# Hybrid encoder layer on one core: the first 256 tokens of each projection in three 256-column matmuls into half a bank

## The chip, the core and the metric

The kernel runs on one core of a Trainium2 chip as one program. The metric is device time in microseconds (us), as the median of several executions. Five engines work side by side and wait for each other through semaphores: PE (TensorE, the matrix multiplier; the trace shows its weight loads apart, as PEld), DVE (VectorE), ACT (ScalarE), POOL (GpSimd) and SP, which issues most of the transfers. PE writes its sums into PSUM, which is cut into banks of 512 fp32 columns on 128 partitions; here eight banks are dealt out by name.

## The reference

One layer of a hybrid encoder is computed for 512 prompt tokens and 64 sample tokens, 576 in all, with a model width of 1024:

```
n = rmsnorm(x);  proj = n @ w_in            (3592 columns: conv input, z, a, b, q, k, v)
oa = gated delta rule over silu(conv(...)), 4 heads;  ob = differential attention, 4 heads
h = x + [oa ; ob] @ w_out
h = h + memory attention(rmsnorm(h) @ w_mem_q, memory K/V) @ w_mem_o
h = h + (relu(rmsnorm(h) @ w_ff1) ** 2) @ w_ff2      (4096 hidden columns)
y = rmsnorm(h)
```

All of it is fp32, and K, V, states and convolution tails are returned too. Every product with a large weight matrix is a *projection* below.

## The kernel before, in words

**Split operands.** A projection does not multiply fp32 by fp32. Weights and activations are each split into a high part, rounded to the format fp32r, and a low part, the rounded remainder: `wh`, `wl` for weights, and the high and low halves of an operand tile `x`. A product is then three fp32r matmuls: wh·x_high, wh·x_low and wl·x_high. ACT makes a high part by a copy, DVE a low part by a subtraction.

**Tiling.** `project` (L175) computes 128 output features at a time for two runs of tokens, `HALVES`: the first 256, then the other 320. For each run it takes one of three PSUM banks named `pr`, loops over the 128-row pieces k of the contraction (eight, or four in the second feed-forward product), and hands the finished bank to an `evac` function. Inside the loop `high_parts` (L191) issues the two products with the high weights, and `low_part` the one with the low weights.

**The first 256 tokens are packed.** The operand tile keeps, for the first 256 tokens, the high part and the low part side by side, 512 columns in a row. So `high_parts` with `a0 == 0` issues *one* matmul of 512 columns over a whole bank: columns 0 to 255 collect wh·x_high, columns 256 to 511 collect wh·x_low. `low_part` adds wl·x_high into columns 0 to 255 with a matmul of 256 columns. The two halves of the bank must therefore be added after the loop. The `evac` functions get the second half as `more`: `add_to` (L202) copies it with ACT and adds with DVE; `add_residual` (L955) adds both halves into the residual with two DVE operations (L960, L962). The other 320 tokens need no such addition: there three matmuls of 320 columns fall on the same columns.

**What sets the order.** Up to the memory attention a planner deals the instructions of each engine from a priority list with its own estimate of durations; work from different stages is interleaved, and the delta rule (small fp32 products in the banks `g0`, `g1`, `gs`) runs between the z, q, k and v projections. The opening stage and the feed-forward stage have their order written out: `segment` (L1191) and a loop at L1483 record each engine's instructions in program order. In the feed-forward stage the first product writes the banks `ba`, `g0`, `g1`, `gs` with 288 columns, and `ff2_block` (L1353), the second product of the group before, is placed between: four wh matmuls, then four wl matmuls per run of tokens.

**The stages in time** (us from the span's start): opening and first convolution blocks to 60; the other convolution blocks to about 100; preparation of the delta rule, with the z projection, to 145; delta rule with q, k, v projections to 285; differential attention to 410; memory K/V and w_out to 480; norm, memory query and memory attention to 593; w_mem_o to 636; feed-forward to 1001; the last second products and the output to the end.

## Time and profile before

| what | value |
|---|---|
| median of 3 runs | 1045.02 us (1044.33 to 1048.94) |
| profiled execution, its own time | 1043.23 us |
| its span in the trace | 1041.4 us |
| PE busy | 1012.3 us, 97% of the span |
| PEld, DVE, ACT, POOL busy | 88%, 69%, 46%, 9% |
| granted PE clock over the span | 0.996 |
| transfers | 89.99 MB, mean 86 GB/s |

A busy PE in this profile is a PE with at least one matmul between its start and its modelled end. Matmuls are pipelined, so the length of one (0.40 us for 512 columns) is more than what it costs in a row of others; the cost in a row is the distance from one start to the next. The releaser behind an idle time is the instruction whose end let the waiting one go.

### The profile page before, as it was taken

To read this page: it belongs to the slowest core of one execution; us is meant where nothing else is said; L and a number is where in the kernel's file an instruction comes from. 1 tells how busy PE (TensorE), PEld (TensorE's weight loads), DVE (VectorE), ACT (ScalarE), POOL (GpSimd) and SP (SyncE) were. 2 spreads that over 40 slices of the span, in tenths; PEclk is the share of its full clock that TensorE was granted. 3 is DMA by queue.
4 is the path that set the end of the run, shared out by engine and by line. 5 is a ranking of instruction groups with operands and counts; after the bars stand their busy time and mean duration, and the time that the engine had idled before them with its cause. 6 is when DMAs were issued, how large, how long until landed. Compare 5 with 4: busy or idle time off the path is not lost.

```text
span 1041.4 us, 17206 instructions
## 1 busy us (share of the span) xinstructions
PE 1012.3 (97%) x6664; PEld 920.2 (88%) x6664; DVE 716.0 (69%) x1548; ACT 479.8 (46%) x995; POOL 92.9 (9%) x138
## 2 busy tenths in 40 slices
PE   8999999999999999999999899999999999999996
PEld 6999889898788877899888699999999999999986
DVE  6766684766467665565555485788888877877684
ACT  6644744333356656444333365634334334334354
POOL 4411120221000000000400000110000000000000
PEclk9999999999999999999999999999999999999999
DMA  7442410200132154625111321223333222223302
GB/s 212 117 127 71 124 41 2 61 1 22 41 103 62 46 208 168 203 82 162 41 41 41 101 63 51 71 82 105 108 93 91 82 82 82 81 82 91 121 2 91
DMA packets 119893, 89.99 MB, mean 86 GB/s; under 512 B 5426, under 2 KB 110000, under 8 KB 119300
## 3 DMA queue, kind: packets, MB, share of 16 engines
q1 hardware_dynamic: 119444, 88.24, 28.1%
q8 instruction: 53, 0.87, 0.4%
q10 hardware_dynamic: 368, 0.66, 0.2%
q14 instruction: 28, 0.23, 0.1%
HBM read 79.14 MB, written 9.74 MB: 85 GB/s over the span
## 4 chain that ended last, share of the span: by engine, by line
PE 86%; issue 5%; DVE 4%; ACT 2%; POOL 1%; DMA 1%; POOLq 0%; ACTq 0%; SPq 0%; DVEq 0%
PE pr L113 50%; PE g L113 15%; PE ba L113 10%; PE gs L113 5%; PE ba L119 3%; PE g L119 2%; POOL tg L217 1%; DMA raw<-in_w_ff_dram 1%; DVE wl L1163 1%; DVE u L960 0%; DVE t L1223 0%; DVE wl L168 0%; DMA out_dram<-p 0%; PE pr L119 0%; ACT p L1044 0%
## 5 line engine op out<-in xcount | busy, mean ns | idle before, releaser
L113 PE MATMUL pr<-x,wh 128*128 128x320 f32 (+1 forms) x1728 | 435.7, 345 | 1.4 <-DVE x L301 0.8
L113 PEld LDWEIGHTS pr<-x,wh 128*128 128x128 f32 x1728 | 291.0, 189 | 22.5 <-issue 1.1
L113 PE MATMUL pr<-x,wl 128*128 128x320 f32 (+1 forms) x1152 | 290.2, 303 | 0.0
L113 PEld LDWEIGHTS pr<-x,wl 128*128 128x128 f32 x1152 | 203.3, 189 | 9.0 <-issue 1.1
L168 DVE TENSOR_TENSOR wl<-raw,wh 128x1024 fp32r<-128x1024 f32 x65 | 80.3, 1236 | 42.1 <-ACT wh L167 41.5
L167 ACT CAST wh<-raw 128x1024 fp32r<-128x1024 f32 x65 | 68.1, 1048 | 63.4 <-PE pr L113 52.7
L960 DVE TENSOR_TENSOR u<-u,pr 128x256 f32<-128x256 f32 (+1 forms) x160 | 71.7, 449 | 19.1 <-PE pr L113 17.0
L1162 ACT CAST wh<-raw 128x512 fp32r<-128x512 f32 (+1 forms) x60 | 43.6, 748 | 66.2 <-PE pr L113 66.1
L1163 DVE TENSOR_TENSOR wl<-raw,wh 128x512 fp32r<-128x512 f32 (+1 forms) x60 | 52.6, 877 | 12.7 <-ACT wh L1162 11.9
L1182 ACT CAST x<-y 128x288 fp32r<-128x288 f32 x64 | 27.7, 433 | 66.4 <-DVE y L1179 65.7
L217 POOL TENSOR_TENSOR tiny<-tiny,nhalf 128x1 f32<-128x1 f32 (+4 forms) x10 | 9.1, 908 | 428.4 <-DVE tiny L1447 325.7
L1175 ACT COPY k<-ba 128x288 f32<-128x288 f32 x42 | 16.7, 397 | 62.9 <-PE ba L113 62.9
L113 PE MATMUL ba<-u,wh 128*128 128x288 f32 x276 | 45.3, 296 | 0.1
L113 PE MATMUL pr<-wh,u 128*128 128x512 f32 x128 | 41.5, 401 | 0.0
L113 PEld LDWEIGHTS ba<-u,wh 128*128 128x128 f32 x276 | 39.4, 188 | 0.6 <-ACT k L1175 0.6
L113 PE MATMUL pr<-x,fh 128*128 128x512 f32 (+1 forms) x168 | 34.1, 338 | 3.2 <-DVE u L962 2.7
L962 DVE TENSOR_TENSOR u<-u,pr 128x256 f32<-128x256 f32 x80 | 33.6, 420 | 2.4
L679 ACT COPY X<-g 128x512 f32<-128x512 f32 (+1 forms) x24 | 13.2, 549 | 42.6 <-PE g L119 42.5
L429 DVE SCALAR_TENSOR_TENSOR p<-p,gcol,p 128x579 f32<-128x579 f32 x33 | 27.1, 821 | 6.4 <-ACT p L427 5.9
L113 PEld LDWEIGHTS pr<-x,fh 128*128 128x128 f32 x168 | 26.5, 188 | 5.0 <-issue 2.3
L1163 DVE TENSOR_TENSOR wl<-t,wh 128x1024 fp32r<-128x1024 f32 x14 | 17.2, 1226 | 20.0 <-ACT wh L1162 20.0
L1185 DVE TENSOR_TENSOR x<-y,x 128x288 fp32r<-128x288 f32 x64 | 28.8, 453 | 1.8
(442 smaller groups left out, 1993.0 us busy)
## 6 DMA issues: line engine op xcount, KB each, us to landing
raw<-in_w_ff_dram SPq DMA_DIRECT2D x32, 512.0 KB
raw<-in_w_in_dram SPq DMA_DIRECT2D x28, 512.0 KB
raw<-in_w_ff_dram SPq DMA_DIRECT2D x56, 256.0 KB
raw<-in_w_mem_k_dram SPq DMA_DIRECT2D x8, 512.0 KB
raw<-in_w_mem_v_dram SPq DMA_DIRECT2D x8, 512.0 KB
raw<-in_w_out_dram SPq DMA_DIRECT2D x8, 512.0 KB
raw<-in_w_mem_q_dram SPq DMA_DIRECT2D x8, 512.0 KB
raw<-in_w_mem_o_dram SPq DMA_DIRECT2D x8, 512.0 KB
```

The costliest lines, as they stand in the source:

```text
L113: i = nc.tensor.matmul(out, lhsT, rhs, start=start, stop=stop, skip_group_check=more)
L119: i = nc.tensor.transpose(out, in_, ident[:n, :n])
L167: A.copy(wh, raw)
L168: V.tensor_tensor(wl, raw, wh.bitcast(F32), ALU.subtract)
L217: G.tensor_tensor(out, in_, bc(nhalf[: in_.shape[0], 0:1], list(in_.shape)), ALU.pow)
L429: V.scalar_tensor_tensor(yv[:, :n], cb[:, i : i + n], cwt[:, m, i : i + 1], yv[:, :n], ALU.mult, ALU.add)
L960: V.tensor_tensor(hm, hm, b, ALU.add)
L962: V.tensor_tensor(hm, hm, more, ALU.add)
L1162: A.copy(wh, src)
L1163: V.tensor_tensor(wl, src, wh.bitcast(F32), ALU.subtract)
L1182: A.copy(piece(sx, 0, k, a0, QN), f)
L1185: V.tensor_tensor(piece(sx, 1, k, a0, QN), f, piece(sx, 0, k, a0, QN).bitcast(F32), ALU.subtract)
```

## The change

For the first 256 tokens `high_parts` now does what it did for the other 320: two matmuls with the high weights, one on x_high and one on x_low, both adding into the same columns. With the low weights' matmul that makes three matmuls of 256 columns into half a bank, where there were one of 512 and one of 256 into a whole one. PE gets 680 matmuls more (6075 before, 6755 after, each with its weight load), over the same number of columns. The second half of the bank and every addition of it are gone: `add_to`, the `more` argument, the second `tensor_tensor` of `add_residual`. DVE issues 108 operations fewer, ACT 25. Silu of z now reads the bank itself.

```diff
     def high_parts(b, w, x, k, a0, n, kt=KT):
         xk = x[k // 4]
-        if a0 == 0:
-            if len(xk.shape) == 4:
-                mm(b.rearrange("p (j n) -> p j n", j=2), w[:, k, :], xk[:, k % 4, :, :256], start=k == 0, stop=k == kt - 1)
-            else:
-                mm(b, w[:, k, :], xk[:, k % 4, :512], start=k == 0, stop=k == kt - 1)
-        else:
-            mm(b[:, :n], w[:, k, :], piece(xk, 0, k % 4, a0, n), start=k == 0, stop=False)
-            mm(b[:, :n], w[:, k, :], piece(xk, 1, k % 4, a0, n), start=False, stop=k == kt - 1)
-
-    def add_to(dst, b, more):
-        A.copy(dst, more)
-        V.tensor_tensor(dst, b, dst, ALU.add)
+        mm(b[:, :n], w[:, k, :], piece(xk, 0, k % 4, a0, n), start=k == 0, stop=False)
+        mm(b[:, :n], w[:, k, :], piece(xk, 1, k % 4, a0, n), start=False, stop=k == kt - 1)
...
             if a0 == 0:
-                add_to(cb[:, 3:259], b, more)
+                A.copy(cb[:, 3:259], b)
...
-            def evac(b, a0, n, more):
-                z = zs[:, h, a0 : a0 + n]
-                if more is not None:
-                    add_to(z, b, more)
-                    b = z
-                A.activation(z, b, AF.Silu)
+            def evac(b, a0, n):
+                A.activation(zs[:, h, a0 : a0 + n], b, AF.Silu)
...
             V.tensor_tensor(hm, hm, b, ALU.add)
-            if more is not None:
-                V.tensor_tensor(hm, hm, more, ALU.add)
...
-            def scaled(b, a0, n, more):
-                q = qh[i][:, a0 : a0 + n]
-                if more is not None:
-                    add_to(q, b, more)
-                    b = q
-                V.tensor_tensor(q, b, rB[:, a0 : a0 + n], ALU.mult)
+            def scaled(b, a0, n):
+                V.tensor_tensor(qh[i][:, a0 : a0 + n], b, rB[:, a0 : a0 + n], ALU.mult)
```

The planner sees other instructions and deals another order in the stages up to the memory attention. Three places matter for the prediction.

First, PE in the last second products of the feed-forward stage, where the order is written out. A row is line, operation, bank<-operand tile,weights, the output's shape, and how many follow each other. Before:

```order
L113 MATMUL pr_10431<-x_6448,wl_10395 128x256 x4
L113 MATMUL pr_10444<-x_6448,wh_10394 128x320 x8
L113 MATMUL pr_10444<-x_6448,wl_10395 128x320 x4
L113 MATMUL pr_10460<-x_6448,wh_10427 128x512 x4
L113 MATMUL pr_10460<-x_6448,wl_10428 128x256 x4
L113 MATMUL pr_10473<-x_6448,wh_10427 128x320 x8
L113 MATMUL pr_10473<-x_6448,wl_10428 128x320 x4
```

In the changed kernel, with new numbers for the same tiles:

```order
L113 MATMUL pr_10948<-x_6803,wl_10909 128x256 x4
L113 MATMUL pr_10964<-x_6803,wh_10908 128x320 x8
L113 MATMUL pr_10964<-x_6803,wl_10909 128x320 x4
L113 MATMUL pr_10980<-x_6803,wh_10944 128x256 x8
L113 MATMUL pr_10980<-x_6803,wl_10945 128x256 x4
L113 MATMUL pr_10996<-x_6803,wh_10944 128x320 x8
L113 MATMUL pr_10996<-x_6803,wl_10945 128x320 x4
```

The row of four matmuls of 512 columns (weights `wh_10427` before, `wh_10944` now) is a row of eight of 256; nothing else moved there.

Second, ACT in the preparation of the delta rule (`B` is the square of k or q, `kdc`, `egl`, `t` are decay factors made by exp, `u_76` receives silu of z; an `ACT_TABLE_LOAD` stands before an activation whose function isn't loaded). Before:

```order
L498 ACT_TABLE_LOAD
L498 ACTIVATE t_1125<-ab 128x20
L508 ACTIVATE egl<-ba_1160 128x20
L576 ACT_TABLE_LOAD
L576 ACTIVATE u_76<-u_76 128x256
L510 ACT_TABLE_LOAD
L510 ACTIVATE kdc<-kdc 128x20
L167 CAST wh_1844<-raw_1842 128x1024
L594 ACTIVATE B_171_1301<-g_169_1294 128x512
L576 ACT_TABLE_LOAD
L576 ACTIVATE u_76<-pr_1764 128x320
L600 ACTIVATE B_173_1309<-g_172_1304 128x512
```

And in the changed kernel (its lines 485, 495, 497, 559, 577, 583, 599 are the lines 498, 508, 510, 576, 594, 600, 616 of before):

```order
L485 ACT_TABLE_LOAD
L485 ACTIVATE t_1216<-ab 128x20
L495 ACTIVATE egl<-ba_1251 128x20
L497 ACTIVATE kdc<-kdc 128x20
L577 ACTIVATE B_171_1392<-g_169_1385 128x512
L583 ACTIVATE B_173_1400<-g_172_1395 128x512
L577 ACTIVATE B_221_1587<-g_219_1580 128x512
L167 CAST wh_1953<-raw_1951 128x1024
L559 ACT_TABLE_LOAD
L559 ACTIVATE u_76<-pr_1867 128x320
L583 ACTIVATE B_223_1595<-g_222_1590 128x512
L599 ACT_TABLE_LOAD
```

The silu and its table load no longer stand between `egl` and `kdc`, so `kdc` needs no load of its own; three squares follow at once, where a cast of weights and another table load stood between the first and the second.

Third, DVE where the feed-forward stage ends: `fl` is the low part of the weights of a block, `x` a low part of the hidden activations, `u_4536<-u_4536,pr_10361` the addition of a bank into the residual. Before:

```order
L1163 TENSOR_TENSOR fl_10336<-raw_10260,fh_10335 128x512
L1185 TENSOR_TENSOR x_6449<-y_10329,x_6449 128x288
L1283 TENSOR_TENSOR y_10333<-y_10333,ba_10220 128x288
L1179 SCALAR_TENSOR_TENSOR y_10333<-y_10333 128x288
L1185 TENSOR_TENSOR x_6449<-y_10354,x_6449 128x288
L1185 TENSOR_TENSOR x_6449<-y_10333,x_6449 128x288
L960 TENSOR_TENSOR u_4536<-u_4536,pr_10361 128x256
L962 TENSOR_TENSOR u_4536<-u_4536,pr_10361 128x256
L1401 TENSOR_TENSOR u_10375<-raw_1755_10235,u_10374 128x512
```

In the changed kernel (L1134, L1156, L937, L1372 are L1163, L1185, L960, L1401 of before) the second addition is gone, and the rest stands as it did:

```order
L1134 TENSOR_TENSOR fl_10847<-raw_10771,fh_10846 128x512
L1156 TENSOR_TENSOR x_6804<-y_10840,x_6804 128x288
L1254 TENSOR_TENSOR y_10844<-y_10844,ba_10731 128x288
L1150 SCALAR_TENSOR_TENSOR y_10844<-y_10844 128x288
L1156 TENSOR_TENSOR x_6804<-y_10865,x_6804 128x288
L1156 TENSOR_TENSOR x_6804<-y_10844,x_6804 128x288
L937 TENSOR_TENSOR u_4731<-u_4731,pr_10872 128x256
L1372 TENSOR_TENSOR u_10889<-raw_1755_10746,u_10888 128x512
```

One row of the residual's addition is left per bank.

More of the change, by code (lines that the diff above doesn't have):

```diff
@@ L454, in hybrid_layer_kernel @@
             high_parts(b, wab2, xs, k, a0, n)
[L455 to L458 removed]
+        V.tensor_copy(abT[:, a0 : a0 + n], b[:16, :n])
     b = bank()
@@ L793, in diff_project, with evac @@
         for kind, base in (("q", 2056), ("k", 2568), ("v", 3080)):
-            def evac(b, a0, n, more):
+            def evac(b, a0, n):
                 ts_ = slice(a0, a0 + n)
@@ L798, in evac @@
                         R = slice(64 * c, 64 * c + 64)
-                        if more is not None:
-                            add_to(qz[h % 2][R, c, ts_], b[R], more[R])
-                        else:
-                            (A.copy if c else V.tensor_copy)(qz[h % 2][R, c, ts_], b[R])
+                        (A.copy if c else V.tensor_copy)(qz[h % 2][R, c, ts_], b[R])
                     return
                 d = small("zr", [P, 320])[:, :n] if kind == "v" else kdT[:, h, ts_]
-                if more is not None:
-                    add_to(d, b, more)
-                else:
-                    V.tensor_copy(d, b)
+                V.tensor_copy(d, b)
                 bt = bank()
@@ L955, in add_residual, with evac @@
     def add_residual(m, last, split=None, g0=None, alone=None):
-        def evac(b, a0, n, more):
+        def evac(b, a0, n):
             hm = hT[m // 4][:, m % 4, a0 : a0 + n]
             V.tensor_tensor(hm, hm, b, ALU.add)
-            if more is not None:
-                V.tensor_tensor(hm, hm, more, ALU.add)
             if not last:
@@ L1021, in hybrid_layer_kernel @@
         for i in range(2):
-            def scaled(b, a0, n, more):
-                q = qh[i][:, a0 : a0 + n]
-                if more is not None:
-                    add_to(q, b, more)
-                    b = q
-                V.tensor_tensor(q, b, rB[:, a0 : a0 + n], ALU.mult)
+            def scaled(b, a0, n):
+                V.tensor_tensor(qh[i][:, a0 : a0 + n], b, rB[:, a0 : a0 + n], ALU.mult)
             project(
@@ L1373, in evac @@
             def evac(a0=a0, n=n):
-                add_residual(m, False)(v[a0][:, :n], a0, n, None if a0 else v[a0][:, 256:])
+                add_residual(m, False)(v[a0][:, :n], a0, n)
                 ends[m] = nc.cur_bb.bb.instructions[-1]
@@ L1404, in last_block, with evac @@
         hi, lo = (view(u, m // 4, 16, P)[:, 4 * (m % 4) : 4 * (m % 4) + 4] for u in wlast)
-        def evac(b, a0, n, more):
-            add_residual(m, True, alone=alone)(b, a0, n, more)
+        def evac(b, a0, n):
+            add_residual(m, True, alone=alone)(b, a0, n)
             hm = hT[m // 4][:, m % 4, a0 : a0 + n]
```

14 lines of the change are left out of this document (5 added, 9 removed).

## The prediction

> **What bounds the kernel now.** The page first: busy time by engine, and the clock.
>
> ```profile
> PE 1012.3 (97%) x6664; PEld 920.2 (88%) x6664; DVE 716.0 (69%) x1548; ACT 479.8 (46%) x995; POOL 92.9 (9%) x138
> PEclk9999999999999999999999999999999999999999
> ```
>
> PE is at work nearly all the time, at full clock. Whether a stage has room is seen in the windows view (length, then busy us and instructions of PE, PEld, DVE, ACT, POOL):
>
> ```profile
> 0.00:25.00 25.00, 20.09 (x99) 15.34 (x100) 16.76 (x27) 16.04 (x30) 11.63 (x26) 1.00 0.78 208
> ...
> 100.00:145.00 45.00, 42.32 (x288) 38.65 (x287) 34.59 (x96) 29.32 (x46) 8.91 (x8) 0.96 0.35 102
> 145.00:410.00 265.00, 260.34 (x1804) 222.97 (x1803) 172.28 (x446) 127.81 (x333) 28.70 (x27) 1.00 0.22 66
> 410.00:480.00 70.00, 70.00 (x404) 63.49 (x403) 40.83 (x68) 29.90 (x49) 0.00 (x0) 1.00 0.48 143
> ...
> 515.00:593.00 78.00, 74.48 (x394) 59.03 (x393) 40.67 (x124) 25.62 (x73) 0.00 (x0) 1.00 0.18 55
> ...
> 700.00:980.00 280.00, 280.00 (x1936) 271.68 (x1935) 223.80 (x428) 108.11 (x201) 1.75 (x1) 1.00 0.29 89
> 980.00:1017.00 37.00, 34.38 (x219) 31.75 (x218) 27.58 (x64) 18.46 (x40) 0.21 (x1) 1.00 0.17 51
> 1017.00:1041.40 24.40, 16.16 (x120) 15.28 (x118) 9.98 (x23) 9.96 (x18) 1.34 (x2) 0.90 0.29 97
> sum 1041.40, PE 1012.31 PEld 920.19 DVE 715.98 ACT 479.78 POOL 92.87; mean PE 92.03 PEld 83.65 DVE 65.09 ACT 43.62 POOL 8.44
> ```
>
> PE idles 1041.40 − 1012.31 = 29.1 us: 4.9 in the opening, 8.2 in the last 24 us, and 16.0 in between. In 410 to 480 and 700 to 980 it idles not at all, and both are full of projections. So whatever a PE instruction costs more there is paid in full, and what DVE and ACT save can win back at most those 16.0 us.
>
> **What 680 more matmuls cost.** No column is added (1 × 512 is 2 × 256), so the price is that of cutting one matmul in two. The largest group of those that are cut, shapes kept apart:
>
> ```profile
> L113 PE MATMUL pr<-x,wh 128*128 128x512 f32 x576 | 198.6, 403 | 0.8 <-DVE x L301 0.8
> ```
>
> With the smaller groups of other weight tiles it is the build's 680. The mean of 0.40 us is an end-to-end length; the price is the distance between starts. In the feed-forward stage four equal ones follow each other (start, length of the merged row, shape, count):
>
> ```profile
> 700.71 1.08 PE L113 MATMUL pr<-x,wh 128*128 128x512 f32 x4
> 701.62 0.64 PE L113 MATMUL pr<-x,wl 128*128 128x256 f32 x4
> 702.10 1.34 PE L113 MATMUL pr<-x,wh 128*128 128x320 f32 x8
> 703.27 0.75 PE L113 MATMUL pr<-x,wl 128*128 128x320 f32 x4
> ```
>
> Four of 512 take 701.62 − 700.71 = 0.91 us, 228 ns each; four of 256 take 0.48 us, 120 ns; eight of 320 take 1.17 us, 146 ns. From 256 to 320 a column costs 26/64 = 0.41 ns, so 120 ns hold some 15 ns that don't depend on the columns. Cutting costs 2 × 120 − 228 = 12 ns; with starts rounded to 10 ns I read 10 to 13. In `project` the shapes alternate instead:
>
> ```profile
> 59.67 0.40 PE L113 MATMUL pr<-x,wh 128*128 128x512 f32 x1
> 59.91 0.28 PE L113 MATMUL pr<-x,wl 128*128 128x256 f32 x1
> ...
> 61.08 0.40 PE L113 MATMUL pr<-x,wh 128*128 128x512 f32 x1
> ```
>
> Four pairs take 61.08 − 59.67 = 1.41 us, 352 ns a pair. Three of 256 at 120 take 360, so here a cut costs 8 ns. Of the 680, 224 lie in the second feed-forward products and the other 456 alternate, or nearly: 224 × 12 + 456 × 8 = 2.7 + 3.6 = 6.3 us; 5.5 to 6.5 by rounding, and I take 6.0. The bound above is the whole fixed part for each, 680 × 15 = 10.2 us, if nothing of it is hidden; below, 680 × 7 = 4.8. Almost none of it is covered: only the opening's 24 cuts stand beside waits, 0.3 us at most.
>
> The Trainium skill ("TensorE: Matmul & The Clock Gate", Back-to-back issue gap) gives warm matmuls N/2.4 + 2.5 ns from start to start, so a cut would cost 2.5 ns and all of them 1.7 us. The 120 ns of the rows stand against 109 by that rule, so the rows decide.
>
> **What leaves ACT and DVE.** Of the additions go 41 pairs of an ACT copy and a DVE addition, and 80 second additions of the residual. Prices, and who waits for the end of the last:
>
> ```profile
> L203 ACT COPY u<-pr x8: 361/373/393, 105.9 to 352.3; 128x256 f32<-128x256 f32 x8
> L204 DVE TENSOR_TENSOR u<-pr,u x8: 400/418/426, 106.3 to 353.9; 128x256 f32<-128x256 f32 x8
> L962 DVE TENSOR_TENSOR u<-u,pr x80: 411/421/424, 433.8 to 1013.1; 128x256 f32<-128x256 f32 x80
>   PE pr L113: 2.7, 2
> ```
>
> That is 121 × 0.42 = 51 us of DVE (some copies come back), yet only 2.7 us of PE's waiting ended with L962, in two places:
>
> ```profile
> 679.97 0.42 DVE L962 TENSOR_TENSOR u<-u,pr 128x256 f32<-128x256 f32 x1
> 680.53 0.68 PE L113 MATMUL pr<-x,fh 128*128 128x320 f32 x3 [0.59 <-DVE u L962]
> ...
> 991.75 0.41 DVE L960 TENSOR_TENSOR u<-u,pr 128x256 f32<-128x256 f32 x1
> 992.20 0.42 DVE L962 TENSOR_TENSOR u<-u,pr 128x256 f32<-128x256 f32 x1
> 992.77 1.41 PE L113 MATMUL pr<-x,fh 128*128 128x320 f32 x8 [2.10 <-DVE u L962]
> ...
> 593.91 0.56 PE L113 MATMUL pr<-x,wh 128*128 128x320 f32 x2 [0.58 <-DVE u L960]
> ```
>
> At the first two DVE is late with other work ahead of the addition, which stays. Without L962 the bank is free 0.45 us sooner at each: −0.9 us; at the third, where an L960 stands behind two others and an L962, I take 0.4. Taken: −1.3 (bounds 0 and −3.3).
>
> **What the planner's new order does.** The largest wait of PE in the planned stages is in the preparation of the delta rule. The chain of waits there:
>
> ```profile
> 117.09 1.28 ACT L510
> 118.60 0.94 ACT wh L167
> 120.05 1.28 ACT L576
> 121.35 0.44 ACT u L576
> 122.76 0.27 ACT u L203
> 123.06 0.42 DVE u L204
> 130.31 1.14 DVE At L623 x4
> ```
>
> ```profile
> 131.49 0.71 PE L113 MATMUL g<-u,u 128*128 128x128 f32 x4 [2.09 <-DVE At L623]
> ```
>
> The rows with no tile name are table loads, 1.28 us each. In the new order the load before `kdc` is gone, and the cast `wh`, the load before silu and silu itself come after the squares; the copy and the addition at 122.76 are gone altogether. That is 1.28 + 0.94 + 1.28 + 0.44 + 0.27 + 0.42 = 4.6 us less ahead of `At`, against a wait of 2.09. Some of the loads return later on, before the exp of the second chunk, and PE comes to that point a little sooner too, since the new order has 55 projection matmuls between the sums of `gg` and this one where there were 58. Late next are POOL's two powers in the same chain, which stay. So the wait goes mostly: −1.5 (bounds 0 and −2.7, with a wait of 0.6 before it).
>
> PE also changes less often between fp32r projections and fp32 work, 368 times in the new order against 378. What a change costs:
>
> ```profile
> 278.49 0.31 PE L113 MATMUL pr<-x,wl 128*128 128x320 f32 x1
> 278.73 1.08 PE L113 MATMUL gs<-on,X 64*64 64x128 f32 x8
> ```
>
> 0.24 us from start to start in place of 0.147: 0.09 more. Ten fewer are −0.5 us at 0.05 to 0.1 each (bounds 0 and −1). Everywhere else between 145 and 410 I count the new order as neutral: the 4.7 us of idle there have many small causes, and can shrink or grow by a few us; that goes into the range.
>
> **Sum.** 1043.23 (profiled execution's own time) + 6.0 − 1.3 − 1.5 − 0.5 = 1045.9. The median of the runs, 1045.02, lies 1.8 above that execution, so the forecast is **1047.7 us**, 0.26% slower. From the bounds: 1043.23 + 4.8 − 7.0 + 1.8 = 1042.8, and 1043.23 + 10.2 + 1.8 = 1055.2.
>
> **Rivals.** *Nothing is won back.* The waits are set by something other than what is removed (the DMA that lands late ahead of 992, POOL's powers ahead of `At`), and a cut costs its whole fixed part of 15 ns. Then 1045.02 + 10.2 = 1055.2. For it: PE idles little and for many reasons. Against it: alternating pairs cost 8 ns more, not 15.
>
> *The new order opens gaps.* In the planned stages ACT and DVE lose work that filled time, small chains stand closer together, and PE meets new waits as large as the present ones, 4.7 us in 145 to 410 (265 − 260.34) plus 2.7 in 100 to 145: 1045.02 + 6.0 − 1.3 + 7.4 = 1057. For it: nearly every row of these stages moves. Against it: no chain gains an operation, and silu's loses one copy and one addition.
>
> *Weight loads bind.* PEld is busy 271.68 of 280 us in the feed-forward stage, 140 ns a load. If that is throughput, 224 more loads there take 31.4 us and find 8.3: 1045 + 23 = 1068. Against it: the four of 256 start every 120 ns with a load each, and runs of twelve would need no more. The Trainium skill ("Perfetto Trace Analysis", Identifying the Most-Contended Engine) judges TensorE by just this busy share of weight loads. By that rule this stage is at its limit before the change.
>
> *Faster.* Banks are freed one or two operations sooner everywhere, and ACT and DVE run ahead. If that takes two thirds of the 16.0 us of idle in the middle, the time is 1045.02 + 6.0 − 0.5 − 10.7 = 1039.8; it is from that share on that the change is 0.5% faster. Against it: the most idle stage, 515 to 593 (78 − 74.48 = 3.5 us), has its longest wait at the softmax's scaling, where no addition stands:
>
> ```profile
> 584.22 0.41 PE L119 MATMUL ba<-ident,p 128*128 128x128 f32 x2 [2.04 <-DVE p L1047]
> ```
>
> **How the numbers follow.** Forecast 0.66, nothing won back 0.13, gaps 0.11, weight loads 0.03, faster 0.07. A measurement of this kernel can tell about 0.5%, 5.2 us, from no change: above 1050.2 or below 1039.8. Most of the second to fourth case is slower by more (0.23 of 0.27). The forecast's own range is 1044 to 1051, by the bounds of its terms with the likelier sides, and 0.03 of it lies over the line. Faster comes from its case alone, 0.07. That makes 0.26 for slower and leaves 0.67 for within. The range 1042 to 1055 leaves out the loads, most of the gaps and the faster case.
>
> **What would show it.** In the trace after: `wl` and `wh` of 256 starting every 120 ns, in runs of twelve too, a feed-forward block of 80 matmuls longer by 0.15 to 0.2 us after growing to 96; the stretch that is now 700 to 980 longer by 2 to 2.7 us with PE never idle; the waits before L962 smaller by 0.4 us; the wait for `At` gone. It would be wrong if 256 alone cost 130 ns or more in a run (+7 us and up), if the idle of PE in the planned stages grew by more than 4 us, or if it fell there by as much as the cuts cost.

## The result: 0.29% slower, and the profile after

The changed kernel takes 1048.59 us (median of 22 executions, 1046.72 to 1049.59), the kernel before 1044.97 us (22 executions beside them, 1042.21 to 1048.94). The ratio is 1.0029, 95% interval 1.0020 to 1.0038: about 3.0 us slower (the ratio compares all executions; the medians alone differ by 3.6). The forecast was +2.7 us to 1047.7, within 0.5%. The time came out where it was put, but, as the experiments show, the terms behind it did not: the cuts (one matmul of 512 columns made into two of 256) were put too high, the wait for `At` won nothing in the end, the removed additions were worth more, and the new order, counted as neutral, cost nearly as much as the whole change.

The profiled execution after took 1048.98 us, with a span of 1046.9. Its page, busy time by engine:

```profile
PE 1018.8 (97%) x7344; PEld 957.9 (91%) x7344; DVE 675.7 (65%) x1440; ACT 472.5 (45%) x970; POOL 95.9 (9%) x138
```

PE has 680 instructions more, DVE 108 and ACT 25 fewer, as the diff says. The windows view, by the stages that the prediction used (length; busy us and instructions of PE, PEld, DVE, ACT, POOL; granted clock, share of DMA, GB/s):

```profile
100.00:145.00 45.00, 42.02 (x325) 39.56 (x324) 37.06 (x103) 29.68 (x45) 8.79 (x10) 1.00 0.36 102
145.00:410.00 265.00, 259.30 (x1883) 227.83 (x1882) 165.90 (x432) 121.54 (x316) 30.61 (x27) 1.00 0.22 64
...
515.00:593.00 78.00, 75.09 (x436) 61.77 (x434) 38.86 (x119) 23.51 (x68) 0.00 (x0) 0.98 0.20 61
...
700.00:980.00 280.00, 280.00 (x2113) 280.00 (x2112) 206.39 (x381) 107.09 (x200) 1.82 (x1) 1.00 0.29 89
```

In 700 to 980 PEld (weight loads, whose ends are modelled as those of the matmuls are) is now busy without a break, 280.00 of 280 us, and PE still never idles. In 515 to 593 the granted clock is 0.98 where it was 1.00. That small digit turns out to matter.

The 256-column matmuls themselves, first in a `project` block, then in the feed-forward stage (start, length, shape, count):

```profile
59.55 0.40 PE L113 MATMUL pr<-x,wh 128*128 128x256 f32 x2
59.79 0.28 PE L113 MATMUL pr<-x,wl 128*128 128x256 f32 x1
59.91 0.40 PE L113 MATMUL pr<-x,wh 128*128 128x256 f32 x2
...
755.48 1.11 PE L113 MATMUL pr<-x,fh 128*128 128x256 f32 x8
756.43 0.63 PE L113 MATMUL pr<-x,fl 128*128 128x256 f32 x4
756.90 1.34 PE L113 MATMUL pr<-x,fh 128*128 128x320 f32 x8
```

Two of them take 59.79 − 59.55 = 0.24 us, eight 756.43 − 755.48 = 0.95 us: 120 ns each in both, with a weight load each. And PE's three waits of which the prediction spoke, with one more, in the timeline:

```profile
129.30 1.16 PE L113 MATMUL g<-u,u 128*128 128x128 f32 x8 [1.22 <-DVE At L606]
...
588.12 0.41 PE L119 MATMUL ba<-ident,p 128*128 128x128 f32 x2 [2.04 <-DVE p L1018]
...
998.00 1.44 PE L113 MATMUL pr<-x,fh 128*128 128x320 f32 x8 [1.55 <-DVE u L937]
```

The wait for `At` went from 2.09 to 1.22 us, that behind the residual near 993 from 2.10 to 1.55, the one at 680 is gone. The softmax's wait of 2.04 us stands as it was. Close behind the wait for `At` there is a new one, which the kernel before does not have:

```profile
133.79 1.09 PE L119 MATMUL ba<-ident,u 128*128 128x128 f32 x8 [0.85 <-DVE u L235]
```

A wait only tells where PE stood still. To see where the time went, the two timelines are compared place by place: at which time does the same instruction start? The table gives it for the kernel before, and how much later (+) or earlier (−) the changed kernel and six of the experiments below reach it, each in its profiled execution. A place is the start of a run of equal matmuls.

| first or last run of a kind | before, us | after | f1 | f3 | f4 | g3 | g2 |
|---|---|---|---|---|---|---|---|
| sums of `gg` (`ba<-gg,triu`) | 114.31 | +0.50 | +0.12 | +0.60 | −0.87 | +0.17 | +0.35 |
| first `gs<-vb,X` of the delta rule | 170.96 | −2.44 | −0.05 | +0.02 | −1.07 | −2.20 | −2.07 |
| its last `gs<-on,X` | 278.73 | +0.51 | +0.19 | +0.06 | −0.90 | −2.25 | −1.84 |
| first `ba<-ident,an` | 330.06 | +2.75 | +0.73 | −0.09 | −0.45 | −2.17 | −1.30 |
| last `ba<-ident,an` | 400.89 | +2.67 | +0.80 | −0.05 | −0.40 | −2.18 | −1.23 |
| `ba<-ident,cols`, behind w_out | 492.00 | +3.37 | +1.30 | +0.36 | −0.40 | −2.22 | −0.77 |
| last memory scores (`ba<-u,kd`) | 584.47 | +3.89 | +1.44 | +0.40 | −0.47 | −2.21 | −0.81 |
| column sums (`pr<-ones,acc`) | 648.35 | +5.21 | +2.58 | +2.27 | −0.96 | −2.21 | −0.98 |
| second `g<-u,f4h` | 697.54 | +3.81 | +1.18 | +2.23 | −2.47 | −2.21 | −2.39 |
| 14th `g<-u,f4h` | 981.98 | +5.85 | +3.22 | +4.25 | −2.51 | −2.22 | −0.35 |
| `ba<-ones,acc`, ahead of the output | 1031.31 | +5.54 | +2.83 | +4.36 | −3.08 | −2.21 | −0.60 |

In f1, f3, f4, g3 and g2 every instruction stands in the order of the kernel before, but for two places in g3 and g2, so the same work stands ahead of each place. The changed kernel has another order, and there a place is a fair comparison only where the same work has been done. That holds from 401 us on, but not before: between the sums of `gg` and the first `gs<-vb,X` PE runs 129 projection matmuls, against 149 in f1, whose work is the same; 12 of 320 and 8 of 256 columns come later. At 146 and 120 ns each that is 2.7 us of work put off, and from there to the first `ba<-ident,an` 18 of 320 and 8 of 256 are made up for, 3.6 us.

With that, the column "after" shows four things. It is 2.9 us earlier at 171 than at 114, but 2.7 of them are work put off; what is won around `At` comes to 0.2 us. From 171 to 330 it falls back by 5.2 us, 3.6 of them that work, and at 492, with the same work done, it is 3.4 us behind, where f1 is 1.3 behind. Some 1.3 us go between 584 and 648. In the feed-forward stage 1.4 us are won before 698 and 2.0 lost to the cuts. The experiments take these apart.

### The profile page after: what moved, and what is told of

Same layout as the page of the kernel before. It is cut to its first block, busy times and chain, and to the rows that moved or that the text cites. A ratio compares the mean times of both kernels' runs of the same rounds, so it can differ in the third digit from the quotient of the medians.

```text
span 1046.9 us, 18372 instructions
## 1 busy us (share of the span) xinstructions
PE 1018.8 (97%) x7344; PEld 957.9 (91%) x7344; DVE 675.7 (65%) x1440; ACT 472.5 (45%) x970; POOL 95.9 (9%) x138
## 4 chain that ended last, share of the span: by engine, by line
PE 86%; DVE 5%; issue 4%; ACT 2%; POOL 2%; DMA 1%; POOLq 0%; ACTq 0%; SPq 0%; DVEq 0%
PE pr L113 51%; PE g L113 14%; PE ba L113 10%; PE gs L113 5%; PE ba L119 3%; PE g L119 2%; DMA u<-in_cache_mem_k_dram 1%; POOL tg L207 1%; DVE wl L168 1%; DMA raw<-in_w_ff_dram 1%; DVE B L631 0%; POOL tiny L207 0%; DVE u L235 0%; POOL Y L600 0%; DVE wl L1134 0%
## 5 line engine op out<-in xcount | busy, mean ns | idle before, releaser
L113 PE MATMUL pr<-x,wh 128*128 128x256 f32 (+1 forms) x2304 | 444.5, 302 | 1.2 <-ACT x L1039 0.5
L113 PEld LDWEIGHTS pr<-x,wh 128*128 128x128 f32 x2304 | 353.9, 190 | 7.3 <-issue 2.7
L113 PE MATMUL pr<-x,wl 128*128 128x320 f32 (+1 forms) x1152 | 286.4, 299 | 0.0
L113 PEld LDWEIGHTS pr<-x,wl 128*128 128x128 f32 x1152 | 197.9, 190 | 1.2 <-issue 0.2
L937 DVE TENSOR_TENSOR u<-u,pr 128x256 f32<-128x256 f32 (+1 forms) x160 | 71.9, 450 | 45.6 <-PE pr L113 44.9
L167 ACT CAST wh<-raw 128x1024 fp32r<-128x1024 f32 x65 | 68.1, 1048 | 67.1 <-PE pr L113 56.9
L1134 DVE TENSOR_TENSOR wl<-raw,wh 128x512 fp32r<-128x512 f32 (+1 forms) x60 | 52.6, 877 | 13.0 <-ACT wh L1133 12.2
L113 PE MATMUL pr<-x,fh 128*128 128x256 f32 (+1 forms) x224 | 34.7, 297 | 1.9 <-DVE u L937 1.6
L113 PEld LDWEIGHTS pr<-x,fh 128*128 128x128 f32 x224 | 31.3, 188 | 2.6 <-DVE u L937 1.9
L1134 DVE TENSOR_TENSOR wl<-t,wh 128x1024 fp32r<-128x1024 f32 x14 | 17.2, 1225 | 19.9 <-ACT wh L1133 19.9
L1156 DVE TENSOR_TENSOR x<-y,x 128x288 fp32r<-128x288 f32 x64 | 28.8, 453 | 1.8
L113 PE MATMUL g<-u,qz 128*128 128x256 f32 (+4 forms) x96 | 29.4, 408 | 0.0
```

The costliest lines, as they stand in the source:

```text
L113: i = nc.tensor.matmul(out, lhsT, rhs, start=start, stop=stop, skip_group_check=more)
L167: A.copy(wh, raw)
L937: V.tensor_tensor(hm, hm, b, ALU.add)
L1134: V.tensor_tensor(wl, src, wh.bitcast(F32), ALU.subtract)
L1156: V.tensor_tensor(piece(sx, 1, k, a0, QN), f, piece(sx, 0, k, a0, QN).bitcast(F32), ALU.subtract)
```

## The experiments

### First set: parts of the change, in the order that the planner deals for each

**e1_ff2_only.** The change in the second feed-forward products alone: 224 cuts, 56 second additions gone. Their order is written out, so the planner isn't touched.

```diff
-                    high_parts(b, v["w"][0], (sx,), k, a0, n, 5)
+                    high_parts(b, v["w"][0], (sx,), k, a0, n, 5, True)
-                add_residual(m, False)(v[a0][:, :n], a0, n, None if a0 else v[a0][:, 256:])
+                add_residual(m, False)(v[a0][:, :n], a0, n, None)
```

The last argument of `high_parts` is a new one that gives it the form of the change.

> The change only in the second feed-forward products (224 of the 680 cuts and 56 of the 121 additions), whose order is written out, so the planner moves nothing. Theory (a cut costs a fixed 11 ns, the traces after show 6.40 us for a block of 40 and 0.043 us more for a feed-forward block; a bank freed one addition sooner takes 0.45 us off two waits): +2.4 - 0.9 = +1.5 us. Rival, nothing is won back: +2.4 us. Rival, weight loads bind: +20 us or more.

Measured: 1048.59 us, ratio 1.0019 (1.0000 to 1.0038). Place by place the cuts cost +2.05 us from 698 to 982 (+2.4 was expected for all 224), the period of 16 cuts being 0.173 us longer, 10.8 ns a cut; and 1.4 us are won from 648 to 698, more than the 0.45 that was put on the wait there. The rest of its difference lies where nothing was edited. It reaches the sums of `gg` 1.65 us later than the kernel before, so one profile against another can differ by that much in the opening alone. At the end of the feed-forward stage its windows view shows this, with the granted clock third from the end:

```profile
985.00:990.00 5.00, 5.00 (x40) 5.00 (x39) 2.13 (x5) 0.67 (x2) 0.00 (x0) 1.00 0.92 292
990.00:995.00 5.00, 2.63 (x17) 2.14 (x15) 1.96 (x5) 1.85 (x5) 0.00 (x0) 0.91 0.30 77
995.00:1000.00 5.00, 3.81 (x15) 3.74 (x15) 4.35 (x10) 5.00 (x11) 0.00 (x0) 0.50 0.00 0
```

A transfer landed 4 us later than in the profile before (2.1 of them this kernel's own lateness), PE idled 2.37 us, and then ran at half clock for 6.8 us: +3.5 us between 982 and 1016. So one execution of a kernel can differ from another by more than the whole effect, through the clock, and places are compared here and not only totals. The last section shows that most of the spread of the kernel before, 1042 to 1049 us, goes with the clock.

**e2_cuts_only.** All 680 cuts, but x_low's products still go to the second half of the bank, and all additions stay.

```diff
-            if len(xk.shape) == 4:
-                mm(b.rearrange("p (j n) -> p j n", j=2), w[:, k, :], xk[:, k % 4, :, :256], start=k == 0, stop=k == kt - 1)
-            else:
-                mm(b, w[:, k, :], xk[:, k % 4, :512], start=k == 0, stop=k == kt - 1)
+            for j in range(2):
+                mm(b[:, 256 * j : 256 * j + 256], w[:, k, :], piece(xk, j, k % 4, 0, 256), start=k == 0 and j == 0, stop=k == kt - 1 and j == 1)
```

> All 680 cuts, but x_low still goes to the second half of the bank and every addition stays. Theory (cuts cost 224 x 10.8 + 456 x 6.9 ns, the additions' removal won the rest back): +5.6 us, 4 to 8 with what the planner moves. Rival, the additions' removal pays nothing and the cut is cheaper on the path than in the rows: the same +3.0 us as the whole change.

Measured: 1064.79 us, ratio 1.0179 (1.0152 to 1.0205), far outside. The cuts in the feed-forward stage cost the same 0.173 us a period, the waits behind L962 stay, but between 114 and 330 the kernel falls back by 22 us. Some 10 of them are projections that this order has done by then and the old one has not (21,888 columns, at 146 ns for 320); at 492 us, with the same work done, it is 14.6 us behind, and its waits up to there are 8.9 us longer. PE's waits in that region, 120 to 420 us (sum, times, longest):

```profile
PE g L119 <- DVE vb L637: 3.9, 3, 1.5
PE ba L119 <- DVE tiny L238: 3.0, 1, 3.0
PE gs L113 <- DVE on L736: 2.3, 3, 1.0
```

The planner, given 680 more small instructions, dealt an order in which the delta rule's chains stand worse.

**e3_no_additions.** No cut, and no second half added.

```diff
-            evac(b[:, :n], a0, n, None if a0 else b[:, 256:])
+            evac(b[:, :n], a0, n)
...
-            if more is not None:
-                V.tensor_tensor(hm, hm, more, ALU.add)
```

> No cut, but every addition is left out: the matmul of 512 columns still fills the second half of the bank, which nobody reads, so the product of the high weights with the low part of x is missing from the first 256 tokens. Theory: -2.6 us (whole change +3.0 less cuts +5.6): -1.3 at the bank waits, the rest in the delta rule's preparation. Rival, nothing is won back: 0 within 1 us. Rival, PE's idle time goes by two thirds: -10 us.

Measured: 1046.25 us, ratio 1.0012 (0.9998 to 1.0026). 133 instructions fewer, and it isn't faster: at 354 us it is 11.4 us behind, about half of that projections done earlier (12,864 columns), at 492 us, with equal work, 6.3 behind, and it wins 1.5 us at the feed-forward waits. Again the order.

**e4_z_only.** The change in the z projection alone: 32 cuts, four copies and four additions gone.

```diff
-            project(weights(w2, 1536 + h * P), xs, evac)
+            project(weights(w2, 1536 + h * P), xs, evac, cut=True)
```

> The change only in the z projection (32 cuts, 4 additions): silu reads the bank. Theory: cuts +0.2 us, the wait for At in the delta rule's preparation shrinks or goes, -1 to -2: -1.3 us. Rival, what the chain gains there is lost again before the end of the delta rule, since the matmuls missing ahead of it come later: 0 within 1 us.

Measured: 1048.27 us, ratio 1.0021 (1.0006 to 1.0036). It is 3.05 us ahead at 187 us, 1.4 behind at 279, 2.9 behind at 354. Here too work has moved (6,016 columns of projections fewer ahead of 187, 4,160 more ahead of 354); at 401 us, with equal work, it is 2.7 us behind, just as the whole change is, from an edit of 40 instructions. And 1.66 us are lost between 584 and 648, where this kernel differs from the one before in nothing.

So with this set the prediction's "elsewhere neutral" was the weak point: what an edit costs by itself can't be read while the order moves with it.

### Second set: the same work with the order held

The planner follows dependencies. A chain of issue-order edges from each instruction to the next on its engine leaves it nothing to decide, and a table of numbers (made from the built program) says which comes next:

```diff
+    for i in placed:
+        if i.engine in last:
+            tc.add_manual_dep(i, last[i.engine].name, mybir.DependencyInfo(mybir.DependencyClass.NoSync, mybir.DependencyReason.DATA), reason="in_order")
+        last[i.engine] = i
```

The kernels below have this at the end of the program. That the chain itself costs nothing is seen in g3 below, which stays 2.2 us ahead of the kernel before from 171 to 1031 us. A cut's two halves stand where the 512 stood, a removed addition leaves its place empty.

**f1_change_old_order.** The whole change in the order of the kernel before.

> The whole change, but with every engine's instructions held in the order that the kernel before has: each matmul of 512 stands as its two of 256 in the same place, each addition is left out of its place, nothing else moves. The times in the changed kernel fall into three: cuts (224 x 10.8 + 456 x 6.9 ns = 5.6 us), removed additions, and the planner's new order. Measure: the time from the first sum of gg (114.3 us) to the column sums ahead of the feed-forward (648.4 us): 534.0 us before, 538.8 in the changed kernel; 320 cuts lie in it, 2.2 us. Theory A (the new order is not neutral: it wins some 2 us at the wait for At and loses some 5 elsewhere): that stretch takes 534.0 + 2.2 - 0.7 (copy and addition of z gone from the chain to At) = 535.5 us here, and the wait for At stays near 1.4 us. Rival B (the order is neutral, and the loss is in the cuts and the freed engines themselves): 538 to 539 us as in the changed kernel. In the feed-forward stage both expect the changed kernel's times, with the 1.4 us of waiting behind L962 gone. Time: A 1047 to 1048, B 1048 to 1050.

Measured: 1046.49 us (1046.1 to 1047.62), ratio 1.0003 (0.9989 to 1.0017). From the sums of `gg` to the column sums it took 536.5 us, between A's 535.5 and B's 538 to 539; the wait for `At` stayed near 1.9. In time A holds, with a little less than its 1047 to 1048: the new order costs the change 1.0029 − 1.0003, some 2.7 us, nearly all of its loss. In places it is 2.1 us at 492 (3.4 against 1.3). The last us above A's stretch has a cause of its own: this profile has two stretches of half clock where the kernel before has one. The two long waits of PE, and the windows around them:

```profile
131.40 2.06 PE L113 MATMUL g<-u,u 128*128 128x128 f32 x8 [1.89 <-DVE At L606]
...
585.46 0.66 PE L119 MATMUL ba<-ident,p 128*128 128x128 f32 x2 [2.04 <-DVE p L1018]
```

```profile
131.00:137.00 6.00, 5.60 (x35) 5.60 (x36) 4.88 (x9) 3.87 (x6) 2.65 (x2) 0.72 0.33 87
...
584.00:590.00 6.00, 4.54 (x11) 2.90 (x12) 2.09 (x8) 1.40 (x5) 0.00 (x0) 0.72 0.01 3
```

Behind each, the granted clock over 6 us is 0.72: 6 × 0.28 = 1.7 us lost, 3.4 us at half clock. The kernel before shows the first in its profile and not the second:

```profile
131.00:137.00 6.00, 5.51 (x30) 5.06 (x30) 4.82 (x9) 3.87 (x6) 2.65 (x2) 0.72 0.32 87
...
584.00:590.00 6.00, 5.24 (x21) 3.24 (x22) 2.63 (x10) 1.84 (x6) 0.00 (x0) 1.00 0.01 3
```

**f2_old_work_new_order.** The converse: 512-column matmuls and additions in the order of the changed kernel.

> The converse: the kernel before, with its 512-column matmuls and its additions, but every engine's instructions in the order of the changed kernel (a 512 stands where the second of its two 256 stood, a copy and addition where the eviction stood). Theory A: the stretch from the first sum of gg to the column sums ahead of the feed-forward takes 534.0 + 2.5 or more = 536.5 to 538 us, with the wait for At below 1.5 us and the loss behind it. Rival B: 534.0 +- 0.5. The feed-forward stage is as in the kernel before under both. Time: A 1047 to 1049, B 1045.

Measured: 1061.87 us, ratio 1.0135 (1.0106 to 1.0165). The stretch from the sums of `gg` to the column sums took 546.7 us. B falls, and A's 536.5 to 538 is far too small. 9.0 us more are lost ahead of it, in the convolution blocks, where copy and addition now stand in places made for a single copy: PE waits 2.7 us there for `p`, and the clock is at half from 107.3 to 114.2 us. This profile is the slowest of the six executions (1067.69 us), so its places show more than the median does. So this doesn't price the new order for the changed work; it shows that an order dealt for one set of work costs another set 16 us (1061.87 against 1046.04).

**f3_cuts_old_order.** The cuts of e2_cuts_only in the old order.

> All 680 cuts and all additions, as in e2_cuts_only, but in the order of the kernel before. Theory A: the 20 us that e2_cuts_only lost came from the order that the planner dealt there; here the time is 1044.9 + 5.6 = 1050.5 us, the stretch from gg to the column sums 534.0 + 2.2 = 536.2 (it was 550 in e2_cuts_only). Rival B (the additional matmuls do it, by weight loads or waits): 1060 or more, and the stretch near 550. The waits behind L962 (0.59 and 2.10 us) stay in both.

Measured: 1049.17 us, ratio 1.0034 (1.0019 to 1.0050), against 1064.79 with the same instructions in the planner's order: A. The order alone was worth 15.6 us there. By the table, the cuts cost 0.6 us up to 114, nothing that can be seen from 171 to 401 (88 cuts), 0.41 from 401 to 492, mostly w_out (75 cuts, 5.5 ns each), 0.04 from there to 584, mostly the memory query (65 cuts), 2.0 in the feed-forward stage. From 584 to 648 it loses 1.87, 1.66 of which e4 also lost without any cut there: the clock's fall at 585.

**f4_no_additions_old_order.** Without cuts and without the additions, as e3_no_additions, in the old order.

> No cut, and the additions left out, as in e3_no_additions (the product of the high weights with the low operand is missing for the first 256 tokens), but in the order of the kernel before. This measures what the removed additions are worth by themselves. Theory A: -0.7 us at the wait for At, -1.4 us behind L962, little else: 1042.8 us, the stretch from gg to the column sums 533.3. Rival B (removing work from ACT and DVE wins nothing or loses, as e3_no_additions with 1046.25 suggests): 1045 to 1046, the stretch 538 as there.

Measured: 1040.51 us, ratio 0.9953 (0.9933 to 0.9972), against 1046.25 in the planner's order. B falls, and A was too small: by places the additions are worth 0.87 us in the opening, 0.5 in w_mem_o, 1.5 behind L962 and 0.6 at the end, while 0.5 are lost from 279 to 401: 3.1 in all. The 0.87 are no more than what two profiles can differ by in the opening (e1 above), so 2.2 are sure. The median says 5.5. The clock accounts for the rest: the eight executions had 0.9958 of full clock on average, the 25 of the kernel before beside them 0.9935, and 0.0023 of 1046 us is 2.4 us, an estimate from these numbers. The 1.5 behind L962 are more than that wait's 0.59, since a second wait for DVE in the same group, in the kernel before

```profile
690.31 0.67 PE L113 MATMUL ba<-u,wl 128*128 128x288 f32 x3 [0.35 <-DVE wl L1163]
```

is gone with it.

### Third set: the clock

Both half-clock stretches of f1 follow a wait of about 2 us. If the waits cause them, shortening a wait must take its fall away, with all work kept.

**g1_change_mask_first.** As f1, one exchange on POOL. Rows of its order (`tg_` the powers of chunk 0 and 1, `Y0` the decay of chunk 0 that is masked):

```diff
 L207 TENSOR_TENSOR tg_167_1383<-tg_168_1384,nhalf_84 128x8
+L600 TENSOR_TENSOR Y0_176_1413<-Y0_176_1413,triu_90 128x512
 L207 TENSOR_TENSOR tg_217_1578<-tg_218_1579,nhalf_84 128x8
-L600 TENSOR_TENSOR Y0_176_1413<-Y0_176_1413,triu_90 128x512
```

> As f1_change_old_order (the whole change in the order of the kernel before), with one exchange on POOL: the mask of chunk 0's decay (1.28 us, L600) stands ahead of chunk 1's power (1.65 us, L207) and not behind it. In f1 the mask was ready at 126.6 us (ACT's exp) and started at 128.9, since the power ahead of it waited for its operand until 127.3. Theory A (the wait for At comes from this order on POOL, and the half clock of 131 to 135 us from that wait): the mask starts 2 us earlier, the wait of PE for At falls from 1.89 to 0.3 us or less, no slice around 131 to 135 shows a clock of 0.5, and the stretch from the sums of gg (114 us) to the end of the delta rule's first half (gs<-vb,X, 171 us) is 1.6 to 3.2 us shorter. Time 1046.5 - 2.5 = 1044. Rival B (the clock falls at that place for another reason, and the next wait in the chain takes over): at most 0.5 us shorter, clock 0.5 as before.

Measured: 1044.39 us, ratio 0.9983 (0.9969 to 0.9998). POOL in f1, where the mask stands behind a power that waits for its operand, and in g1:

```profile
127.29 1.65 POOL L207 TENSOR_TENSOR tg<-tg,nhalf 128x8 f32<-128x8 f32 x1 [2.27 <-DVE tg L585]
128.91 1.28 POOL L600 TENSOR_TENSOR Y<-Y,triu 128x512 f32<-128x512 f32 x1
```

```profile
126.77 1.30 POOL L600 TENSOR_TENSOR Y<-Y,triu 128x512 f32<-128x512 f32 x1 [1.63 <-ACT Y L599]
128.17 1.64 POOL L207 TENSOR_TENSOR tg<-tg,nhalf 128x8 f32<-128x8 f32 x1
```

And PE in g1, its wait and the window in which f1 had 0.72:

```profile
129.83 1.16 PE L113 MATMUL g<-u,u 128*128 128x128 f32 x8 [0.21 <-DVE At L606]
```

```profile
131.00:137.00 6.00, 5.24 (x45) 5.02 (x45) 4.90 (x9) 5.09 (x10) 2.05 (x3) 1.00 0.34 87
```

The wait fell from 1.89 to 0.21, the clock stayed at 1.00, and the first `gs<-vb,X` starts 2.1 us earlier: A. What held `At` back was a 1.65 us power that nothing needed yet, in front of the mask.

**g2_change_mask_spread.** In addition, the fillers of the last memory attention head are spread. PE's order (`ba<-p0` the transposes of a softmax block, `ba<-u,kd` the scores of the next, `pr` matmuls of w_mem_o that fill the wait):

```diff
+L119 MATMUL ba_1072_6152<-ident_79,p0_1071_6148 128x128 x2
+L113 MATMUL ba_1073_6157<-u_788_4398,kd_1049_6005 128x256
+L113 MATMUL ba_1073_6157<-u_788_4398,kd_1050_6006 128x256
 L113 MATMUL pr_1106_6305<-x_957_5533,wh_1104_6301 128x256 x2
 L113 MATMUL pr_1106_6305<-x_957_5533,wl_1105_6302 128x256
 L113 MATMUL pr_1106_6305<-x_957_5533,wh_1104_6301 128x256 x2
-L119 MATMUL ba_1072_6152<-ident_79,p0_1071_6148 128x128 x2
-L113 MATMUL ba_1073_6157<-u_788_4398,kd_1049_6005 128x256
-L113 MATMUL ba_1073_6157<-u_788_4398,kd_1050_6006 128x256
...
```

The next block's transposes and scores move ahead of six `pr` matmuls in the same way.

> g1_change_mask_first, and in the last head of the memory attention the matmuls that fill the waits for the softmax stand elsewhere, none added: five of 256 columns go from ahead of the second block's transposes to behind them, six from ahead of the third's to ahead of the fourth's. In f1 PE waited 0.85 us before the third and 2.04 before the fourth; now it should wait some 0.6, 1.0 and 1.3. Theory A (one wait of about 2 us lets the clock fall to half for 3.4 us, shorter ones don't): the slices at 585 to 589 us show full clock, and the stretch from the last memory scores (584 us) to the column sums (648 us) is 1.4 to 1.7 us shorter than in f1 (65.0 us). Time 1.5 us below g1, 1042.5. Rival B (the clock follows the total idle time, which stays 2.9 us): the fall stays, same time as g1.

Measured: 1042.80 us (1042.45 to 1044.16), ratio 0.9979 (0.9965 to 0.9994). PE's waits in g2, and the window at 584:

```profile
576.78 0.41 PE L119 MATMUL ba<-ident,p 128*128 128x128 f32 x2 [0.66 <-DVE p L1018]
580.10 0.41 PE L119 MATMUL ba<-ident,p 128*128 128x128 f32 x2 [0.98 <-DVE p L1018]
583.41 0.41 PE L119 MATMUL ba<-ident,p 128*128 128x128 f32 x2 [1.33 <-DVE p L1018]
```

```profile
584.00:590.00 6.00, 5.46 (x23) 3.12 (x22) 2.56 (x9) 1.70 (x6) 0.00 (x0) 1.00 0.01 3
```

The waits sum to 2.97 us, those of f1 before its blocks to 0.85 + 2.04 = 2.89: PE idles as long as before, but in shorter pieces, and the clock stays at 1.00. The median is 1.6 us below g1's. That is A against B: the idle time in all is not what counts. But it isn't the single wait alone either; g1, without the rearrangement, was at half clock from 582.6 on, in the middle of its wait of 2.04 us, and the last section shows what the falls follow.

**g3_before_mask_spread.** The kernel before with these two rearrangements and nothing else.

> The kernel before with the same two rearrangements (the mask first on POOL, the fillers of the memory attention spread), its 512-column matmuls and its additions as they were. With both half-clock stretches gone, the change is compared without them: g2 against this one. Theory A (cuts cost 3.5 to 4.3 us, the removed additions are worth 3.1): g2 is 0 to 1.5 us slower than this kernel, which takes 1046.0 - 3.5 = 1042.5 or less. Rival B (the removed additions are worth the 5.5 us of f4's median, the cuts 3): g2 is 2 us faster.

Measured: 1040.96 us (1040.52 to 1041.94), ratio 0.9952 (0.9933 to 0.9971). It is faster than both kernels of this case, with the work of the kernel before. And against g2 it gives the change's own price, in the same order and without these falls: 1042.80 − 1040.96 = 1.8 us slower, a little over A's 0 to 1.5; by places it is 1.6.

### What binds in the weight loads

**g4_two_of_160.** The kernel before, with every 320 of the second feed-forward products cut in two.

```diff
-                    high_parts(b, v["w"][0], (sx,), k, a0, n, 5)
+                        for j in range(2):
+                            for p0, pn in ((256, 160), (416, 160)):
+                                mm(b[:, p0 - a0 : p0 - a0 + pn], v["w"][0][:, k, :], sx[:, k, j, p0 : p0 + pn], start=k == 0 and j == 0 and p0 == 256, stop=False)
```

(The products with the low weights likewise.)

> The kernel before, but in the second feed-forward products every matmul of 320 columns (the other 320 tokens) is cut into two of 160, 336 cuts; nothing else changes. It tells whether weight loads would bind: in the changed kernel PEld was busy 280.0 of 280 us from 700 to 980 and PE lost no time. Fixed part and columns (15 + 0.41 x 160 = 81 ns each, against 146 for a 320): 16 ns a cut, +5.4 us. Rival (the loads are at their limit, so 160-column matmuls can't follow each other faster than the 110 to 120 ns of a load): 2 x 115 - 146 = 84 ns a cut, +28 us; if a load needs the 132 ns that PEld's busy time gives, 118 ns a cut, +40 us.

Measured: 1094.83 us, +50.2. The expectation miscounted: 56 blocks of 12 make 672 cuts, not 336. With 672, the fixed part would give 10.8 us and a limit at the loads, at 115 ns, 56. The timeline of g4:

```profile
742.33 1.92 PE L113 MATMUL pr<-x,wh 128*128 128x160 f32 x16
744.08 1.06 PE L113 MATMUL pr<-x,wl 128*128 128x160 f32 x8
744.98 1.13 PE L113 MATMUL pr<-x,wh 128*128 128x512 f32 x4
```

Sixteen take 744.08 − 742.33 = 1.75 us, 109 ns each, where the columns would have allowed 81. That is 2 × 110 − 146 = 74 ns a cut, and 672 × 74 = 49.7 us: all of it. So at 160 columns, each matmul with a weight load of its own, something else than the columns sets 110 ns. That it is the load fits, but no run takes the loads away. If it is, the rival "weight loads bind" was wrong for 256 columns by only some 9 ns each.

## Why the prediction was right, and where it was not

**Cuts, 6.0 us: too large, about 3.3.** The price of 12 ns was read well in the feed-forward stage (10.8 ns), and that of 8 ns fairly from 401 to 492 (5.5 to 7). The step that failed is to take the 8 ns for all of the other 456. From 171 to 401 us PE's time from start to start over the projections, waits left out, grows from 85.44 us in the kernel before to 85.72 in f3, 3 ns for each of the 88 cuts; from 492 to 584 it grows from 57.50 to 57.63, 2 ns for each of 65. In the first stretch PE's waits also shrink, by 0.25 us, in the second by 0.04: so "almost none of it is covered" was wrong too, but by little. Why a cut costs so little where projections alternate with other work stays open. The total is from f3, without the fall at 585 that it has (1.66) and with the one at 132 that it lacks (0.6 by the table): 4.36 − 1.66 + 0.6 = 3.3.

**Evictions, −1.3: too small, −2.2 to −3.1.** At 680 the changed kernels won 1.4 to 1.5 us, not 0.45: with DVE freed, the wait at 690 in the same group goes too. Near 993 the wait fell by 0.55, as forecast, and the wait at 593 was right in size, 0.5. At the end (0.57), and perhaps in the opening (0.87), something was won where I had put nothing.

**The wait for `At`, −1.5: right for the chain, and nothing won.** `At` is ready 2.2 us earlier (131.49 to 129.30), but PE also comes to it sooner, since of the work in between 7 matmuls of 320 and 6 of 256 columns, 1.7 us, now come later. "A little sooner", read from 55 matmuls where there were 58, missed this, since the 55 are the smaller ones. So the wait fell by 0.87 only, and new waits of 0.85 and 0.34 us follow before 171. I named POOL's powers as what is late next; g1 shows that one of them was the cause.

**"Everywhere else between 145 and 410 I count the new order as neutral": the step that failed most.** At 492 us, with the same work done, the changed kernel is 3.4 us behind and f1, the same work in the old order, 1.3: the new order costs 2.1 us up to there. PE's waits from 114 to 492 us, added up from the timelines, are 8.6 us after and 7.1 in f1, which is most of it. That is the rival "new order opens gaps" in its place, at a small part of its 7.4 us: from 145 to 410 PE's idle time grew from 4.7 to 5.7 us. Ten fewer switches, −0.5 us, can't be seen in any run.

**The sum.** 6.0 − 1.3 − 1.5 − 0.5 = +2.7 was forecast, +3.0 measured. By the runs: work +1.8 (g2 against g3), or +0.3 (−1.2 to +1.8) by f1 with the falls in it, and the new order the rest, 2.7 by f1. The parts don't add up exactly: by places the cuts (+3.3) and the additions (−3.1) alone give +0.2, both together in g2 against g3 +1.6. The 3.0 hold one thing more that nobody forecast: the 22 executions of the changed kernel ran at 0.9962 of full clock on average, the 77 of the kernel before that stand beside the experiments at 0.9939. By that the change was spared 2.4 us of half clock (0.0023 × 1046, an estimate), since its waits fall otherwise. The hit in time was a compensation, and so luck.

**Rivals.** "Weight loads bind" falls, since PE took 177 loads more (2112 for 1935) in a stretch whose PEld was busy 271.68 of 280 us, and lost only the 10.8 ns a cut; the reason that I gave, 256s in short runs at 120 ns, held in runs of twelve. The Trainium skill ("Perfetto Trace Analysis", Identifying the Most-Contended Engine) takes this busy share, beside the share of peak FLOPs, as the measure of how near TensorE is to its limit; in this trace the busy share left no room and the loads found it. Nor do the 2.5 ns for the fixed part ("TensorE: Matmul & The Clock Gate" of the Trainium skill, Back-to-back issue gap) agree with the 10.8 ns a cut; that section itself calls its formula the isolated gap and says that weight loads and matmuls together set the spacing in a stream, so the prediction used it outside its range. "Nothing is won back" and "faster" fall with the numbers above.

**What was to be seen.** The 120 ns, a block longer by 0.173 (0.15 to 0.2 forecast), 2.0 us more in 698 to 982 with PE never idle, and the smaller waits behind the residual all came. The wait for `At` did not go, but fell from 2.09 to 1.22. And the profile before was 1.7 us below its median, which I added to the sum as a constant; it is one of the executions with a granted clock of 0.996, which took 1042.7 to 1045.0 us, and the median mixes them with others that ran at 0.991 to 0.994.

## What to carry to other kernels

When a planner sets the order, an edit has two prices, that of its work and that of the order dealt for it, and the second can be the larger: the same instructions took 1064.8 us in one order and 1049.2 in another. Hold the order while you price the work, and compare the starts of the same instructions in both timelines instead of totals. Where the orders differ, count the work that stands ahead of such a place first: most of what looked like a gain at `At`, and of its loss behind, was work moved from one side of the mark to the other. A long wait of PE may cost more than its length: look at the clock in the window behind it, and break it into shorter ones if it can't be removed.

## What the runs showed of the hardware

**Half clock after 2 us of waiting, by steps of 3.41 us.** The softmax's wait of 2.04 us stands in twelve of the fourteen profiles; in eight of them the granted clock fell to 0.50. In six kernels PE waited 1.89 to 2.09 us for `At`, and in five of them the clock fell. Behind the residual at the end of the feed-forward stage eight profiles wait 1.86 to 2.37 us, and three fell. Behind the waits for `At` of 1.2 us (after, e3, e4), and at both rearranged places in g2 and g3, where the longest wait is 1.3 us, none did. A fall often lasts 3.4 us and costs 1.7.

Why the same wait does it in one execution and not in another can be read from the clock's record in the traces. Each of the 19 falls ahead of the last 20 us, in all fourteen profiles, begins a whole number of steps of 3.413 us (26 to 293 of them) after the clock first rose to full. Cut the time into these steps, and add up PE's idle time in each, by the modelled ends of its matmuls. Of 4150 steps at full clock 17 hold 1.89 us of idle time or more, and half clock follows all of them; 4126 hold 1.67 or less, and it follows none; of the 7 between, from 1.69 to 1.82, it follows two. So what counts is the idle time within one step, about half of it, and a wait of 2 us does it when the step's edge doesn't divide it. In the kernel before, the step with the wait for `At` and the next, then the two that share the softmax's 2.04 us:

```profile
128.80:132.21 3.41, 1.32 (x10) 1.01 (x9) 1.90 (x7) 2.57 (x4) 1.47 (x2) 1.00 0.04 16
132.21:135.63 3.42, 3.42 (x13) 3.03 (x13) 2.38 (x5) 3.39 (x6) 2.65 (x2) 0.50 0.24 58
...
579.36:582.77 3.41, 1.95 (x10) 1.17 (x9) 1.54 (x6) 0.83 (x3) 0.00 (x0) 1.00 0.17 56
582.77:586.19 3.42, 1.97 (x8) 1.42 (x9) 1.51 (x6) 0.84 (x4) 0.00 (x0) 1.00 0.03 5
```

The first step has 3.41 − 1.32 = 2.09 us of idle time and half clock behind it, the other two have 1.46 and 1.45, and none. In the changed kernel the softmax's wait lies within one step:

```profile
585.32:588.74 3.42, 1.38 (x8) 0.96 (x7) 1.44 (x5) 0.94 (x4) 0.00 (x0) 1.00 0.00 0
588.74:592.15 3.41, 3.41 (x7) 1.72 (x6) 1.45 (x5) 0.65 (x3) 0.00 (x0) 0.50 0.02 5
```

This also explains most of the spread of the kernel before. Of its 77 executions beside the experiments, the 37 with a granted clock of 0.996 or 0.998 took 1042.4 to 1045.0 us, the 14 at 0.992 to 0.994 took 1044.3 to 1046.5, and the 26 at 0.991 took 1047.3 to 1049.6. With both waits shortened the executions of g3 lie within 1.4 us.

The Trainium skill ("TensorE: Matmul & The Clock Gate", What's actually happening) has the clock halved after an idle window of about 3.4 us that runs freely. The steps agree with that window, but here 1.89 us of idle time in it always sufficed. The advice of the Trainium skill of no gaps above about 3 us (the same page, Why this matters for your kernels) is too wide here: waits of 1.89 us for `At` in f1, and of 1.69 us in f2, were enough.

**110 ns at 160 columns.** From one matmul to the next, each with its own 128x128 weights, 160 columns took 110 ns, 256 took 120, 320 took 146. PEld's busy share does not show it, since it was at 100% with 256 columns at no loss beyond the 10.8 ns a cut.
